# All modulation vectors through TensorE in four column groups, and a first FFN whose products begin with half of the scale

## Chip, cores and metric

The kernel runs on one core of a Trainium2 chip. The metric is device time in microseconds (us), the median of several executions. Six things work side by side on the core: TensorE (PE in the rows; its weight loads are PEld), VectorE (DVE), ScalarE (ACT), GpSimd (POOL), SyncE (SP, which issues nearly all DMAs) and the DMA engines. Every engine takes its own instructions strictly in the order in which the program lists them.

## Reference

One step of a two-layer trunk on 384 tokens (128 of a prompt, 256 of a sample), width 1024, all in float32. Each layer adds three branches to the residual x, every one with a norm that a conditioning modulates:

```python
mod = (jnp.einsum('bd,de->be', jax.nn.silu(cond), lp['w_ada']) + lp['b_ada']).reshape(cond.shape[0], N_MOD, 1, D_MODEL)
h = rms_norm(x, lp['norm_g'][0]) * (1.0 + mod[:, 1]) + mod[:, 0]
x = x + 0.5 * mod[:, 2] * swiglu(h, lp['ffn_w_gate'][0], lp['ffn_w_up'][0], lp['ffn_w_down'][0])
h = rms_norm(x, lp['norm_g'][1]) * (1.0 + mod[:, 4]) + mod[:, 3]
mix, state = token_mix(h, lp, l, cache)
x = x + mod[:, 5] * mix
h = rms_norm(x, lp['norm_g'][2]) * (1.0 + mod[:, 7]) + mod[:, 6]
x = x + 0.5 * mod[:, 8] * swiglu(h, lp['ffn_w_gate'][1], lp['ffn_w_up'][1], lp['ffn_w_down'][1])
```

`swiglu` is `silu(h @ w_gate) * (h @ w_up) @ w_down` with a hidden width of 2816. There are nine modulations of 1024 a layer, each for two conditionings (prompt and sample): `w_ada` is 1024 x 9216 for each layer, 37.7 MB a layer. The four mixers are not touched by the change.

## The kernel before, in words

**Layout.** Activations lie feature-major: 8 blocks of 128 features, 384 tokens in the free dimension. A large product is made with three fp32r matmuls (`mm3`, L184 to L188): weight and activation are split into a high and a low part (`whi`, `wlo`; `hhi`, `hlo`), and high by high, high by low and low by high are added in PSUM. The split costs one cast on ScalarE (L169) and one subtraction on VectorE (L173; GpSimd for a few) for each 128 x 1024 unit of weights. TensorE can't begin the third of the three before `wlo` is there.

**FFN.** There are four, called FFN 1 to 4 here: two in each layer, before and behind the mixers. One has a gate/up stage (44 units of 24 matmuls, tiles `pg` and `pu`, 1056 matmuls) and a down stage (tile `pd`, 528 matmuls). Weights come in MB pieces (`raw`, three buffers).

**Modulations.** All but five quarters run beside TensorE (`ada`, L258 to L292): a quarter is 256 of a modulation's 1024 columns, 1 MB of `w_ada`. For the prompt's conditioning, VectorE multiplies and adds eight blocks (L268, L271); for the sample's, ScalarE multiplies (L269, L274) and GpSimd adds (L275). Two 32 x 32 transposes (L278), two sums (L279) and, once for a group of quarters, four products with selection matrices (L285) bring the result to columns. These jobs are woven into the FFNs by `hook`: 28 quarters in FFN 1, 20 in FFN 2, 16 in FFN 3, none in FFN 4. The five others (`ada_rows`, L238 to L255) use TensorE at the start: the conditioning is the stationary operand (128 x 2), 256 columns of `w_ada` move, eight plain-fp32 products to a quarter (L246), then two transposes.

**Start.** The first norm needs modulation 1 (scale) and 0 (shift) of layer 0. `start` (L372) runs through `ORDER`: quarters of scale on TensorE, quarters of shift on the other engines, and between them the scaled residual `xs` (L345, L346). The first FFN's first ten products (`EARLY`) use `xs` with two extra columns that hold the shift (`early_shift`, L327), so that 386 columns move; the product is multiplied by 1/rms and shifted behind it (`hidden`, L194). So the first of them waits for the whole scale and the whole shift.

**Order.** The program is written in Python against a scheduler that simulates the engines' time and lists the instructions of each engine by it; jobs from `hook` carry a raised priority. What it lists is fixed before the launch.

Of the kernel before, what the change touches and what calls it, by code (L numbers as in the profile page):

```python
# [8 lines left out]
F32 = mybir.dt.float32  # L9
# [8 lines left out]
D = 1024  # L18
# [16 lines left out]
K_ID, K_SEL, K_ONE = 0, 128, 640  # L35
# [8 lines left out]
ORDER = "nsrsrsrrr"  # L44
RING, NT1, NT2 = 256 * 310, 6, 4
# [4 lines left out]
def host_constants():  # L50
# [12 lines left out]
    for r in range(4):  # L63
        c[:, K_SEL + 128 * r:K_SEL + 128 * (r + 1)] = i[None, :] == (32 * r + i[:, None] % 32)
# [15 lines left out]
def pack_vectors(x):  # L80
    """The small vectors of both layers as columns of 128."""
    import numpy as np

    rows = [x["c_ctx"].reshape(8, 128), x["c"].reshape(8, 128)]
    for l in range(2):
        rows += [x["norm_g"][l].reshape(24, 128), x["b_ada"][l].reshape(72, 128), x["dn_conv_w"][l].reshape(18, 128)]
        rows += [np.tile(x[n][l], 2)[None] for n in ("dn_norm_g", "da_norm_g", "ml_norm_g", "ret_norm_g")]
        rows.append(np.repeat(x["ret_decay_logit"][l].reshape(4, 2), 64, axis=1))
    return np.ascontiguousarray(np.concatenate(rows, 0).T)
# [6 lines left out]
def lockstep(*tasks):  # L96
    """Issue several tasks a stage of each at a time."""
# [5 lines left out]
class Ring:  # L103
    """Tiles at consecutive offsets of one window of memory, each over the oldest ones."""
# [13 lines left out]
class Trunk:  # L118
# [75 lines left out]
    def hidden(self, w, name="mm"):  # L194
        """A product with the normed residual; the first ones are scaled by 1 / rms and shifted behind the product."""
# [9 lines left out]
        nc.vector.tensor_copy(b, ps[:, T:T + 2])  # L205
        t = self.ring.tmp([128, T], "hn")
# [6 lines left out]
    def setup(self):  # L213
# [10 lines left out]
        nc.scalar.activation(out=self.cond, in_=vec[:, 0:16], func=AF.Silu)  # L224
        xrs = []
# [12 lines left out]
    def ada_rows(self, l, quarters):  # L238
        """Quarters of the nine modulations on the tensor engine, for both conditionings."""
        nc = self.nc  # L240
        cond = self.cond.rearrange("p (s k) -> p k s", s=2)
        for mod, j in quarters:
            raw = self.wcols(self.I["w_ada"][l], mod * D + 256 * j)
            ps = self.pm.tile([2, 256], F32, tag="mm", name="arow")
            for kk in range(KD):
                nc.tensor.matmul(ps, cond[:, kk], raw[:, kk], start=(kk == 0), stop=(kk == KD - 1))  # L246
            row = self.ring.tmp([2, 256], "mrow")
            nc.scalar.copy(row, ps)
            tp = self.mxps([128, 2, 2])
            for q in range(2):  # L250
                nc.tensor.transpose(tp[:, q], row[:, 128 * q:128 * q + 128], self.k(K_ID)[0:2, 0:2])
            c = slice(8 * mod + 2 * j, 8 * mod + 2 * j + 2)
            nc.vector.tensor_tensor(self.mods[l][:, :, c].rearrange("p s k -> p k s"), tp,
                                    self.prm[l][:, R_B:R_B + 72][:, c].unsqueeze(2).to_broadcast([128, 2, 2]),
                                    op=ALU.add)  # L255
            yield

    def ada(self, l, mod, n=4):  # L258
        """The same beside the tensor engine, n quarters from a modulation on, one at a time."""
        nc = self.nc  # L260
        ap = self.ap
        xa = ap.tile([128, 2, 8 * n], F32, tag="xa", name="xa", bufs=1)
        for j in range(n):
            raw = ap.tile([128, KD, 256], F32, tag="araw", name="araw", bufs=2)
            c0 = mod * D + 256 * j
            nc.sync.dma_start(raw, self.I["w_ada"][l, :, c0:c0 + 256].rearrange("(k p) n -> p k n", p=128))
            acc = [ap.tile([128, 256], F32, tag="acc", name="acc", bufs=6) for _ in range(2)]
            nc.vector.tensor_scalar_mul(acc[0], raw[:, 0], self.cond[:, 0:1])  # L268
            nc.scalar.mul(acc[1], raw[:, 0], self.cond[:, 8:9])  # L269
            for kk in range(1, KD):  # L270
                nc.vector.scalar_tensor_tensor(  # L271
                    acc[0], raw[:, kk], self.cond[:, kk:kk + 1], acc[0], op0=ALU.mult, op1=ALU.add)
                t = ap.tile([128, 256], F32, tag="acc", name="acct", bufs=6)
                nc.scalar.mul(t, raw[:, kk], self.cond[:, 8 + kk:9 + kk])  # L274
                self.last_add = nc.gpsimd.tensor_tensor(acc[1], acc[1], t, op=ALU.add)  # L275
            for s in range(2):
                tr = ap.tile([128, 256], F32, tag="acc", name="accr", bufs=6)
                nc.vector.transpose(tr, acc[s])  # L278
                nc.vector.tensor_reduce(  # L279
                    xa[:, s, 8 * j:8 * j + 8], tr.rearrange("p (a b) -> p a b", b=32), axis=AX, op=ALU.add  # L280
                )
            yield
        ps = self.mxps([128, 2, 2 * n])
        for r in range(4):
            nc.tensor.matmul(  # L285
                ps, self.k(K_SEL + 128 * r), xa.rearrange("p s (k r) -> p s k r", r=4)[:, :, :, r],
                start=(r == 0), stop=(r == 3),
            )
        c = slice(8 * mod, 8 * mod + 2 * n)
        nc.vector.tensor_tensor(self.mods[l][:, :, c], ps,  # L290
                                self.prm[l][:, R_B:R_B + 72][:, c].unsqueeze(1).to_broadcast([128, 2, 2 * n]), op=ALU.add)
        yield  # L292

# [8 lines left out]
    def norm_begin(self, l, n):  # L302
        """The statistics of the next norm gather while the residual is updated."""
# [22 lines left out]
    def early_shift(self):  # L326
        """Two columns beside the scaled residual, for the shift of the two streams behind the product."""  # L327
# [30 lines left out]
    def rstd(self):  # L358
        """1 / rms of every token, on all partitions."""
# [12 lines left out]
    def start(self):  # L372
        """The first norm, as the input and the quarters of its modulation come in."""
        self.norm_begin(0, 0)
        for kk in range(KD):
            self.norm_square(kk)
        self.early_open()
        shift, rows = self.ada(0, 0, ORDER.count("s")), self.ada_rows(
            0, [(1, j) for j in range(4)] + [(0, j) for j in range(ORDER.count("s"), 4)])
        j = 0  # L380
        for c in ORDER:
            if c == "n":
                self.rstd()
            elif c == "s":
                next(shift)
            else:
                next(rows)
                if j < 4:
                    self.scales(0, 0, self.nx[2], 2 * j, 2 * j + 2)
                    self.early_part(2 * j, True)  # L390
                    self.early_part(2 * j + 1, True)
                j += 1
        next(shift)
        self.early_shift()
        with self.after(self.last_add):
            for k in range(KD):
                self.norm_scale(k)
# [1087 lines left out]
```

## Time and profile before

| | us |
|---|---|
| median of 3 runs (2241.5 to 2248.05) | 2246.99 |
| span of the profiled execution | 2244.0 |
| start, up to the first product of FFN 1 | 48.6 |
| FFN 1, gate/up and down | 215.8 + 118.2 |
| FFN 2 | 216.3 + 111.3 |
| FFN 3 | 200.5 + 91.6 |
| FFN 4 | 186.0 + 94.8 |

The span runs from the first to the last instruction; the timed runs hold 3.0 us more by their median. Between the FFNs lie the mixers of layer 0 and layer 1. A view of stretches gives, for each, its length, then the busy time (and the instructions) of PE, PEld, DVE, ACT and POOL, the granted TensorE clock as a share of 2.4 GHz, the DMA share and GB/s. Matmuls overlap in TensorE's pipeline: one lasts twice as long as the distance to the next, so the distance between starts is read, not the duration. A plain-fp32 product stands in the trace as two MATMULs, two passes. An fp32r product is one.

### The profile page before, as it was taken

The numbers are of one execution on the slowest core, as the hardware profiler recorded it, in microseconds if no ns is written. First come the engines' busy times: TensorE is split into PE (matmuls) and PEld (weight loads), VectorE is DVE, ScalarE is ACT, GpSimd is POOL, SyncE is SP. The second block draws the span as 40 slices with busy tenths as digits, with TensorE's granted clock in tenths as the row PEclk, the third lists the DMA queues.
The fourth block names the chain that finished last, engine by engine and source line by source line (L and its number), as shares of the span: only waits on it lengthen the run. The fifth ranks groups of instructions, "written<-read, shape, count | busy, mean of one in ns | idle before, by whom it ended". The sixth has DMA issues, their size and how long they took to land. (4 is left out here: it accounts for less than half of the span.)

```text
span 2244.0 us, 33102 instructions
## 1 busy us (share of the span) xinstructions
PE 2076.3 (93%) x12150; PEld 1992.7 (89%) x12150; DVE 1724.6 (77%) x3198; ACT 1039.3 (46%) x1978; POOL 942.2 (42%) x855
## 2 busy tenths in 40 slices
PE   6988888999789997998998999999987999999999
PEld 3988788999679997998887999998976899999999
DVE  8999998778995469999899974467999745764433
ACT  5666554634234235765556643354333332463322
POOL 5556666433655237366476520134354531500000
PEclk8999999999889999999999999999998999999999
DMA  9466655444333244566555644344442321444342
GB/s 306 152 217 199 202 198 164 129 136 105 83 81 103 60 164 155 169 210 214 186 193 155 206 135 133 128 146 137 119 95 83 109 76 59 160 134 129 115 139 76
DMA packets 316515, 323.08 MB, mean 144 GB/s; under 512 B 42112, under 2 KB 287296, under 8 KB 315840
## 3 DMA queue, kind: packets, MB, share of 16 engines
q1 hardware_dynamic: 316080, 320.70, 46.1%
q8 instruction: 95, 1.56, 0.3%
q14 instruction: 68, 0.56, 0.1%
q10 hardware_dynamic: 272, 0.26, 0.0%
HBM read 313.25 MB, written 7.69 MB: 143 GB/s over the span
## 5 line engine op out<-in xcount | busy, mean ns | idle before, releaser
L169 ACT CAST whi<-raw 128x1024 fp32r<-128x1024 f32 x422 | 440.2, 1045 | 511.1 <-PE mg L187 133.3
L173 DVE TENSOR_TENSOR wlo<-raw,whi 128x1024 fp32r<-128x1024 f32 x324 | 434.8, 1343 | 226.9 <-ACT whi L169 223.8
L275 POOL TENSOR_TENSOR acc<-acc,acct 128x256 f32<-128x256 f32 x469 | 440.5, 939 | 334.7 <-ACT acct L274 306.4
L173 POOL TENSOR_TENSOR wlo<-raw,whi 128x1024 fp32r<-128x1024 f32 x98 | 244.9, 2505 | 289.9 <-ACT whi L169 244.2
L271 DVE SCALAR_TENSOR_TENSOR acc<-araw,cond,acc 128x256 f32<-128x256 f32 x469 | 323.5, 690 | 6.3
L274 ACT ACTIVATE acct<-araw,cond 128x256 f32<-128x256 f32 x469 | 214.1, 501 | 139.7 <-DVE accr L278 83.4
L188 PE MATMUL pd<-hh,wlo 128*128 128x384 f32 x704 | 240.8, 345 | 20.2 <-DVE wlo L173 20.2
L186 PE MATMUL pd<-hh,whi 128*128 128x384 f32 x704 | 240.5, 342 | 9.0 <-ACT whi L169 4.5
L187 PE MATMUL pd<-hl,whi 128*128 128x384 f32 x704 | 239.9, 341 | 0.0
L188 PE MATMUL pg<-hhi,wlo 128*128 128x384 f32 x544 | 184.8, 340 | 19.2 <-DVE wlo L173 19.0
L188 PE MATMUL pu<-hhi,wlo 128*128 128x384 f32 x544 | 184.7, 340 | 13.4 <-DVE wlo L173 13.1
L186 PE MATMUL pg<-hhi,whi 128*128 128x384 f32 x544 | 182.1, 335 | 0.4 <-ACT whi L169 0.4
L187 PE MATMUL pu<-hlo,whi 128*128 128x384 f32 x544 | 182.2, 335 | 0.0
L186 PE MATMUL pu<-hhi,whi 128*128 128x384 f32 x544 | 182.2, 335 | 0.0
L187 PE MATMUL pg<-hlo,whi 128*128 128x384 f32 x544 | 182.1, 335 | 0.0
L186 PE MATMUL mg<-hhi,whi 128*128 128x384 f32 x512 | 177.7, 347 | 0.0
L187 PE MATMUL mg<-hlo,whi 128*128 128x384 f32 x512 | 175.4, 343 | 0.0
L188 PE MATMUL mg<-hhi,wlo 128*128 128x384 f32 x512 | 174.5, 343 | 0.5 <-DVE wlo L173 0.5
L321 POOL TENSOR_SCALAR xg<-xT,gs 128x128 f32<-128x128 f32 (+1 forms) x96 | 101.9, 1074 | 150.9 <-DVE xT L432 150.8
L188 PEld LDWEIGHTS pd<-hh,wlo 128*128 128x128 f32 x704 | 134.0, 191 | 27.6 <-DVE wlo L173 27.6
L186 PEld LDWEIGHTS pd<-hh,whi 128*128 128x128 f32 x704 | 134.4, 191 | 11.3 <-ACT whi L169 5.4
L187 PEld LDWEIGHTS pd<-hl,whi 128*128 128x128 f32 x704 | 134.5, 191 | 0.1
(410 smaller groups left out, 4961.5 us busy)
## 6 DMA issues: line engine op xcount, KB each, us to landing
araw<-in_w_ada SPq DMA_DIRECT2D x67, 1024.0 KB
raw<-in_w_in SPq DMA_DIRECT2D x62, 1024.0 KB
raw<-in_ffn_w_gate SPq DMA_DIRECT2D x44, 1024.0 KB
raw<-in_ffn_w_up SPq DMA_DIRECT2D x44, 1024.0 KB
raw<-in_ffn_w_down SPq DMA_DIRECT2D x40, 1024.0 KB
raw<-in_w_branch SPq DMA_DIRECT2D x16, 512.0 KB
raw<-in_w_out SPq DMA_DIRECT2D x8, 1024.0 KB
raw<-in_w_ada SPq DMA_DIRECT2D x5, 1024.0 KB
```

Of the source, the lines that this page charges most:

```text
L169: nc.scalar.copy(hi, src)
L173: (eng or nc.vector).tensor_tensor(lo, src, hi.bitcast(F32), op=ALU.subtract)
L186: nc.tensor.matmul(ps, w[0], x[0], start=start, stop=False)
L187: nc.tensor.matmul(ps, w[0], x[1], start=False, stop=False)
L188: nc.tensor.matmul(ps, w[1], x[0], start=False, stop=stop)
L271: nc.vector.scalar_tensor_tensor(acc[0], raw[:, kk], self.cond[:, kk:kk + 1], acc[0], op0=ALU.mult, op1=ALU.add)
L274: nc.scalar.mul(t, raw[:, kk], self.cond[:, 8 + kk:9 + kk])
L275: self.last_add = nc.gpsimd.tensor_tensor(acc[1], acc[1], t, op=ALU.add)
L321: self.nc.gpsimd.tensor_scalar(xg[kk][:, a:e], self.xT[:, kk, a:e], gs[:, s, kk:kk + 1], None, op0=ALU.mult)
```

## The change

Every modulation now goes through TensorE. A half (512 of 1024 columns) is loaded as two 1 MB tiles (`araw`). `pair_rows_times` takes the conditionings as a stationary of 128 x 32 (`cond32`: two columns used, thirty zero) and sends 512 columns of a block of 128 rows past it; block `kk` stands in column group `kk % 4` of the array, 32 columns wide, and writes 32 partitions of one PSUM tile (`arow`). Eight such products make a half, two for each group. ScalarE copies the tile, four transposes (`acol`) turn it, and one sum on VectorE adds the four groups; the bias is added behind. The code of the other engines (`ada`, `ada_rows`, the selection matrices) is gone.

The halves are woven into the FFNs one at each `hook`: 12 in FFN 1, 8 in FFN 2, 10 in FFN 3, 2 in FFN 4. Four stand at the start. There, six units of FFN 1 are begun without the shift columns: the first four blocks of three units when the first half of the scale is known, the other four when the second is, then three whole units; the shift's halves come after them. What the shift adds to these six units is a product of its own, of the raw weights with the shift (`sh32`, again in four column groups, 256 columns), added as a bias behind (`shifted`). The scales of the next norm are computed later, between the two halves of the down stage.

```diff
-K_ID, K_SEL, K_ONE = 0, 128, 640
+K_ID, K_ONE = 0, 128
...
-ORDER = "nsrsrsrrr"
-RING, NT1, NT2 = 256 * 310, 6, 4
+EARLY0 = 6
+RING, NT1, NT2 = 256 * 308, 6, 4
...
+        return self.shifted(ps, b)
+
+    def shifted(self, ps, b):
+        nc = self.nc
...
+        self.cond32 = self.const.tile([128, KD, 32], F32, name="cond32")
+        nc.vector.memset(self.cond32, 0.0)
+        nc.vector.tensor_copy(self.cond32[:, :, 0:2], self.cond.rearrange("p (s k) -> p k s", s=2))
...
-    def ada_rows(self, l, quarters):
...
-    def ada(self, l, mod, n=4):
...
+    def ada_load(self, l, mod, hf):
+        c0 = mod * D + 512 * hf
+        raws = []
+        for i in range(2):
+            raws.append(self.ap.tile([128, 4, 512], F32, tag="araw", name="araw", bufs=self.n_araw))
+            self.last_load = self.nc.sync.dma_start(raws[i], self.I["w_ada"][l, 512 * i:512 * i + 512, c0:c0 + 512].rearrange(
+                "(k p) n -> p k n", p=128))
+        return raws
+    def pair_rows_times(self, cols, blocks, n, out):
+        nc = self.nc
+        ps = self.mxps([128, n], "arow")
+        for kk in range(KD):
+            g = kk % 4
+            nc.tensor.matmul(ps[32 * g:32 * g + 32], cols[:, kk], blocks[kk], start=(kk < 4), stop=(kk >= 4),
+                             tile_position=(0, 32 * g))
+        row = self.ring.tmp([128, n], "mrow")
+        nc.scalar.copy(row, ps)
+        tp = self.mxps([128, n // 128, 128], "acol")
+        for q in range(n // 128):
+            nc.tensor.transpose(tp[:, q], row[:, 128 * q:128 * q + 128], self.k(K_ID))
+        nc.vector.tensor_reduce(out, tp.rearrange("p q (g e) -> p e q g", g=4)[:, 0:2], axis=AX, op=ALU.add)
+    def ada_half(self, l, mod, hf, raws):
+        t = self.small.tile([128, 2, 4], F32, tag="asum", name="asum")
+        self.pair_rows_times(self.cond32, [r[:, g] for r in raws for g in range(4)], 512, t)
+        c = slice(8 * mod + 4 * hf, 8 * mod + 4 * hf + 4)
+        self.nc.vector.tensor_tensor(self.mods[l][:, :, c], t,
+                                     self.prm[l][:, R_B:R_B + 72][:, c].unsqueeze(1).to_broadcast([128, 2, 4]), op=ALU.add)
+    def ada(self, l, *halves):
+        for h in halves:
+            self.ada_half(l, *h, self.ada_load(l, *h))
...
+        wg, wu = I["ffn_w_gate"][0, 0], I["ffn_w_up"][0, 0]
+
+        def cols(w, c0):
+            t = self.ring.tile([128, KD, 256], F32, name="raw0")
+            nc.sync.dma_start(t, w[:, c0:c0 + 256].rearrange("(k p) n -> p k n", p=128))
+            return t
+
+        scale = [self.ada_load(0, 1, 0)]
+        raw = [cols(wg, 0), cols(wu, 0)]
+        scale.append(self.ada_load(0, 1, 1))
+        raw.append(self.wcols(wg, 256))
+        shift = [self.ada_load(0, 0, hf) for hf in range(2)]
+        self.up1 = self.wcols(wu, 256)
+        sh32 = self.ring.tile([128, KD, 32], F32, name="sh32")
+        nc.gpsimd.memset(sh32, 0.0)
+        units = [(0, 0), (1, 0), (0, 1), (1, 1), (2, 0), (2, 1)]
+        w, ps = {}, {}
+
+        def split(u):
+            r, m = u
+            w[u] = self.split_unit(raw[r][:, :, 128 * m:128 * m + 128], [128, KD, 128])
+            ps[u] = (self.mmps if r < 2 else lambda name: self.mxps([128, T], name))(name="pg" if r != 1 else "pu")
+
+        def rows(u, k0, k1):
+            for k in range(k0, k1):
+                self.mm3(ps[u], (w[u][0][:, k], w[u][1][:, k]), [t[:, k, 0:T] for t in self.xs], k == 0, k == KD - 1)
+
+        for hf in range(2):
+            self.ada_half(0, 1, hf, scale[hf])
+            self.scales(0, 0, self.nx[2], 4 * hf, 4 * hf + 4)
+            for k in range(4 * hf, 4 * hf + 4):
+                self.early_part(k, True)
+            if hf == 0:
+                for u in units[:3]:
+                    split(u)
+                    rows(u, 0, 4)
+        for u in units[:3]:
+            rows(u, 4, KD)
+        self.rstd()
+        for u in units[3:]:
+            split(u)
+            rows(u, 0, KD)
+        for hf in range(2):
+            self.ada_half(0, 0, hf, shift[hf])
+        nc.vector.tensor_copy(sh32[:, :, 0:2], self.mods[0][:, :, 0:8].rearrange("p s k -> p k s"))
+        bias = []
+        for r in range(3):
+            bias.append(self.small.tile([128, 2, 2], F32, tag="sb", name="sb", bufs=3))
+            self.pair_rows_times(sh32, [raw[r][:, kk] for kk in range(KD)], 256, bias[r])
...
+        self.ready = [(ps[u], bias[u[0]][:, :, u[1]]) for u in units]
...
+        if (l, n) == (0, 0):
+            self.early = EARLY0
...
+            begun = 2 - j if (l, i) == (0, 0) and j < 2 else 0
+            rg = None if begun else self.wcols(I["ffn_w_gate"][l, i], 256 * j)
+            ru = None if begun == 2 else self.up1 if begun else self.wcols(I["ffn_w_up"][l, i], 256 * j)
...
+                pg = self.shifted(*self.ready.pop(0)) if begun else self.hidden(wg, "pg")
+                pu = self.shifted(*self.ready.pop(0)) if begun == 2 else self.hidden(wu, "pu")
...
-            hook(2)
+            hook(1)
...
+            if nxt is not None and dg == 0:
+                self.scales(*nxt, self.nx[2])
...
+            self.n_araw = 4
...
+            self.n_araw = 3
...
-                self.ffn(l, 0, self.ada(l, 5, 16) if l else chain(self.ada(l, 2, 12), self.ada(l, 5, 16)), (l, 1))
+                mods = {(0, 0): ((0, 2, 8),), (0, 1): ((0, 8, 9), (1, 0, 3)), (1, 0): ((1, 3, 8),), (1, 1): ((1, 8, 9),)}
+                jobs = [chain(*(self.ada(m, *((k, hf) for k in range(a, e) for hf in range(2)))
+                                for m, a, e in mods[l, i])) for i in range(2)]
+                self.ffn(l, 0, jobs[0], (l, 1))
...
-                self.ffn(l, 1, iter(()) if l else self.ada(1, 0, 20), None if l else (1, 0))
+                self.ffn(l, 1, jobs[1], None if l else (1, 0))
```

Where the scheduler puts this: the first place is TensorE at the start (`arow` is a modulation's row tile, `mx` a small product or a transpose, `pg` and `pu` are the FFN's products). Before:

```order
L246 MATMUL arow_386<-raw_384,cond_89 2x256 x8
L246 MATMUL arow_413<-raw_411,cond_89 2x256 x8
L251 MATMUL mx_397<-cst_82,mrow_395 128x2 x2
L251 MATMUL mx_424<-cst_82,mrow_422 128x2 x2
L285 MATMUL mx_428<-xa_182,cst_82 128x12 x4
L186 MATMUL pg_519<-xs_160,whi_511 128x386
```

Now:

```order
L261 MATMUL arow_192<-araw_165,cond32_91 32x512 x4
L261 MATMUL arow_192<-araw_167,cond32_91 32x512 x4
L267 MATMUL acol_203<-cst_82,mrow_201 128x128 x4
L184 MATMUL pg_232<-xs_163,whi_228 128x384
L185 MATMUL pg_232<-xs_164,whi_228 128x384
```

The first FFN product stood behind five quarters and the shift; it now stands behind one half of the scale, whose eight products are in one row.

The second place is TensorE in FFN 1's gate/up stage, where `hook` puts a half. Before:

```order
L187 MATMUL pg_1222<-hlo_461,whi_1214 128x384
L188 MATMUL pg_1222<-hhi_460,wlo_1215 128x384
L186 MATMUL pu_1247<-hhi_460,whi_1218 128x384
L187 MATMUL pu_1247<-hlo_461,whi_1218 128x384
L188 MATMUL pu_1247<-hhi_460,wlo_1219 128x384
```

Now:

```order
L261 MATMUL arow_950<-araw_945,cond32_91 32x512
L184 MATMUL pu_1070<-hhi_572,whi_1041 128x384
L261 MATMUL arow_950<-araw_945,cond32_91 32x512
L185 MATMUL pu_1070<-hlo_573,whi_1041 128x384
L261 MATMUL arow_950<-araw_947,cond32_91 32x512
L186 MATMUL pu_1070<-hhi_572,wlo_1042 128x384
```

A product of 32 columns and one of the FFN's take turns, one by one, until the eight of the half are through.

The third place is VectorE in the same stage. Before:

```order
L173 TENSOR_TENSOR wlo<-raw,whi 128x1024
L271 SCALAR_TENSOR_TENSOR acc<-araw,cond,acc 128x256
L468 TENSOR_TENSOR hl<-sg,hh 128x384
L271 SCALAR_TENSOR_TENSOR acc<-araw,cond,acc 128x256 x2
L278 STREAM_TRANSPOSE accr<-acc 128x256
L173 TENSOR_TENSOR wlo<-raw,whi 128x1024
```

Now:

```order
L493 TENSOR_TENSOR sg<-sg,pu 128x384
L171 TENSOR_TENSOR wlo<-raw,whi 128x1024
L497 TENSOR_TENSOR hl<-sg,hh 128x384
L171 TENSOR_TENSOR wlo<-raw,whi 128x1024
L268 TENSOR_REDUCE asum<-acol 128x8
L274 TENSOR_TENSOR mods_87<-asum,vec 128x2x4
```

The multiply-adds between the splits are gone; one sum and one addition to a half are left.

How the list puts the 256 thin products (32 columns, `w_ada`) of the four FFNs among the full ones:

| | alone between full products | three in a row | five in a row (4 + 1) | eight in a row |
|---|---|---|---|---|
| FFN 1 (12 halves) | 82 | 2 times | | 1 time |
| FFN 2 (8 halves) | 54 | | 2 times | |
| FFN 3 (10 halves) | 72 | | | 1 time |
| FFN 4 (2 halves) | 6 | | 2 times | |

## Rows read from the trace of the kernel before

**Rows 1.** Stretches: length, PE, PEld, DVE, ACT, POOL, clock, DMA; FFN 1 to 4.

```profile
48.60:264.40 215.80, 195.35 (x1066) 185.99 (x1066) 212.04 (x350) 136.75 (x270) 131.77 (x138) 0.99 0.62 197
264.40:382.60 118.20, 102.50 (x537) 97.13 (x537) 109.99 (x182) 63.38 (x116) 79.57 (x86) 0.94 0.57 182
864.80:1081.10 216.30, 194.60 (x1067) 188.00 (x1066) 211.33 (x348) 135.31 (x265) 122.96 (x128) 0.98 0.58 186
1081.10:1192.40 111.30, 97.70 (x538) 93.48 (x537) 99.00 (x161) 58.71 (x109) 69.50 (x73) 0.98 0.60 196
1192.40:1392.90 200.50, 191.65 (x1075) 188.07 (x1074) 155.82 (x256) 106.92 (x197) 66.78 (x66) 0.98 0.49 153
1392.90:1484.50 91.60, 91.60 (x531) 91.60 (x530) 39.28 (x58) 30.75 (x39) 13.84 (x20) 1.00 0.43 129
1958.20:2144.20 186.00, 185.26 (x1067) 184.90 (x1066) 94.81 (x145) 80.22 (x130) 7.90 (x6) 1.00 0.40 125
2144.20:2239.00 94.80, 94.80 (x549) 94.45 (x548) 31.65 (x38) 23.28 (x25) 0.00 (x0) 1.00 0.28 97
```

**Rows 2.** Groups of instructions on DVE during FFN 1: busy us, mean ns, idle before.

```profile
L271 DVE SCALAR_TENSOR_TENSOR acc<-araw,cond,acc 128x256 f32<-128x256 f32 x196 | 135.0, 689 | 2.6
L173 DVE TENSOR_TENSOR wlo<-raw,whi 128x1024 fp32r<-128x1024 f32 x66 | 97.0, 1472 | 0.4 <-ACT whi L169 0.4
```

**Rows 3.** Waits of PE during FFN 1: us in total, times, longest.

```profile
PE pg L188 <- DVE wlo L173: 11.6, 13, 2.1
PE pd L188 <- DVE wlo L173: 11.5, 11, 2.1
```

**Rows 4.** A stretch within FFN 3's down stage, columns as in rows 1.

```profile
1402.50:1458.60 56.10, 56.10 (x325) 56.10 (x324) 23.37 (x30) 17.34 (x22) 7.14 (x8) 1.00 0.39 128
```

**Rows 5.** Timeline, PE: one product with 32 rows of stationary between full ones.

```profile
611.49 0.34 PE L188 MATMUL mg<-hhi,wlo 128*128 128x384 f32 x1
611.76 0.91 PE L1057 MATMUL mx<-bkTs,bqT 32*128 32x384 f32 x2
612.60 0.45 PE L186 MATMUL mg<-hhi,whi 128*128 128x384 f32 x1
612.88 0.34 PE L187 MATMUL mg<-hlo,whi 128*128 128x384 f32 x1
```

**Rows 6.** Timeline, PE: two quarters of a modulation (sixteen products, 32 passes).

```profile
23.24 7.07 PE L246 MATMUL arow<-raw,cond 128*2 128x256 f32 x32
```

**Rows 7.** Groups of weight loads from 20 to 30 us: busy us, mean ns.

```profile
L246 PEld LDWEIGHTS arow<-raw,cond 128*2 128x2 f32 x37 | 3.1, 85 | 4.7 <-issue 0.2
L363 PEld LDWEIGHTS mx<-cst,sqacc 128*128 128x128 f32 x6 | 0.7, 191 | 1.5 <-PE arow L246 1.5
```

**Rows 8.** Timeline, PE: a plain-fp32 product of full width between full ones.

```profile
1101.39 0.45 PE L285 MATMUL mx<-xa,cst 128*128 128x80 f32 x2
1101.56 0.46 PE L186 MATMUL pd<-hh,whi 128*128 128x384 f32 x1
1101.86 0.45 PE L285 MATMUL mx<-xa,cst 128*128 128x80 f32 x2
```

**Rows 9.** Timeline, PE: three products in three row groups, one behind another.

```profile
607.91 0.92 PE L1057 MATMUL mx<-bkTs,bqT 32*128 32x384 f32 x6 [0.37 <-DVE bkTs L1044]
```

**Rows 10.** Timeline, PE: four transposes between full products.

```profile
576.91 0.60 PE L1042 MATMUL mx<-cst,bx 128*128 128x128 f32 x4
577.26 0.42 PE L186 MATMUL mg<-hhi,whi 128*128 128x384 f32 x1
```

**Rows 11.** Stretches of the start, columns as in rows 1.

```profile
0.00:10.00 10.00, 3.50 (x17) 3.12 (x18) 1.78 (x3) 1.50 (x2) 0.19 (x4) 1.00 0.83 275
10.00:20.00 10.00, 5.15 (x20) 2.06 (x19) 9.52 (x15) 6.47 (x15) 5.73 (x7) 0.66 1.10 349
```

**Rows 12.** Timeline, PE: the first FFN product; then a stretch as in rows 1.

```profile
48.60 0.69 PE L186 MATMUL pg<-xs,whi 128*128 128x386 f32 x1 [3.34 <-ACT xs L332]
49.00:69.00 20.00, 19.05 (x97) 18.54 (x97) 19.07 (x37) 13.07 (x31) 17.35 (x16) 0.87 0.55 175
```

More of the change, by code (lines that the diff above doesn't have):

```diff
@@ L62, in host_constants @@
     c[:, K_PB:K_PB + 128] = 128 - i[None, :]
-    for r in range(4):
-        c[:, K_SEL + 128 * r:K_SEL + 128 * (r + 1)] = i[None, :] == (32 * r + i[:, None] % 32)
     c[:, K_KP] = 127 - i
@@ L235, in setup @@
                 nc.vector.tensor_copy(self.xT[:, 4 * hf:4 * hf + 4, 128 * b:128 * b + 128], tp)
-    def ada_rows(self, l, quarters):
-        nc = self.nc
[L241 to L255, printed above, removed]
-            yield
@@ L258, in ada @@
-    def ada(self, l, mod, n=4):
[L260 to L292, printed above, removed]
@@ L372, in start @@
     def start(self):
+        nc, I = self.nc, self.I
         self.norm_begin(0, 0)
@@ L377, in start @@
         self.early_open()
[L378 to L392, printed above, removed]
@@ L393, in start @@
-        next(shift)
-        self.early_shift()
-        with self.after(self.last_add):
-            for k in range(KD):
-                self.norm_scale(k)
+        wg, wu = I["ffn_w_gate"][0, 0], I["ffn_w_up"][0, 0]
[5 more added lines that the diff above has]
+        raw = [cols(wg, 0), cols(wu, 0)]
@@ L398, in start @@
+        self.ready = [(ps[u], bias[u[0]][:, :, u[1]]) for u in units]
+        for k in range(KD):
+            self.norm_scale(k)
         self.norm()
@@ L453, in ffn_body @@
         for j in range(KF // 2):
-            rg = self.wcols(I["ffn_w_gate"][l, i], 256 * j)
-            ru = self.wcols(I["ffn_w_up"][l, i], 256 * j)
+            begun = 2 - j if (l, i) == (0, 0) and j < 2 else 0
+            rg = None if begun else self.wcols(I["ffn_w_gate"][l, i], 256 * j)
+            ru = None if begun == 2 else self.up1 if begun else self.wcols(I["ffn_w_up"][l, i], 256 * j)
             for m in range(2):
                 f = 2 * j + m
-                wg = self.split_unit(rg[:, :, 128 * m:128 * m + 128], [128, KD, 128])
-                wu = self.split_unit(ru[:, :, 128 * m:128 * m + 128], [128, KD, 128])
-                pg = self.hidden(wg, "pg")
-                pu = self.hidden(wu, "pu")
+                wg = None if begun else self.split_unit(rg[:, :, 128 * m:128 * m + 128], [128, KD, 128])
+                wu = None if begun == 2 else self.split_unit(ru[:, :, 128 * m:128 * m + 128], [128, KD, 128])
+                pg = self.shifted(*self.ready.pop(0)) if begun else self.hidden(wg, "pg")
+                pu = self.shifted(*self.ready.pop(0)) if begun == 2 else self.hidden(wu, "pu")
                 sg = self.wp.tile([128, T], F32, tag="nt", name="sg", bufs=2)
@@ L473, in ffn_body @@
             self.norm_begin(*nxt)
-            self.scales(*nxt, self.nx[2])
         g = self.gates(l, 2 * i, 0.5)
```

## The prediction

> **What bounds the kernel now.** I read the stretches of the four FFNs first [rows 1], since they hold 55% of the span and all of the modulation work. All four run the same 1056 and 528 products. Where nothing holds TensorE up, it starts one each 56.1 / 325 = 0.173 us [rows 4]. FFN 4 has no modulation work and takes 186.0 + 94.8 us, with VectorE busy for half of its gate/up stage; the down stage of FFN 3, whose quarters have run out, takes 91.6. So 186.0 + 91.6 = 277.6 us is a clean FFN with a norm behind it. FFN 1 takes 334.0, FFN 2 327.6, FFN 3 292.1: they lose 56, 50 and 15 us. The cause is VectorE: in FFN 1 it is busy for 322 of 334 us, 135.0 of them with the multiply-adds of the quarters, and a split (L173) takes 1472 ns beside them [rows 2]. TensorE waits for the low part of the weights, in the gate/up and in the down stage [rows 3]; the listed waits are less than the loss, because products that start late overlap less. The fourth place is the start: the first FFN product stands at 48.6, after waiting 3.34 us for the shift columns [rows 12]. What the change can win is these 121 us and part of the 48.6.
>
> **What it removes.** The multiply-adds leave VectorE, ScalarE and GpSimd in FFN 1 to 3. With those 196 gone, VectorE has at most 322 - 135 = 187 us of work in FFN 1, and I set the three FFNs at their clean 277.6.
>
> **What it adds: the price of a thin product.** In the listed order 214 of the 256 thin products in the FFNs stand alone between full ones, twice three stand in a row, and six times five or eight. A pass of 256 plain-fp32 columns costs 7.07 / 32 = 0.22 us [rows 6], so two passes of 512 cost 0.88, whether 2 or 128 columns of the array are used. Four groups would share that only if their products stood side by side. The nearest thing in the trace to a thin product between full ones is one with 32 rows of stationary [rows 5]: from the full product before it to the one behind the next there are 612.88 - 611.49 = 1.39 us where two distances of 0.173 would have been 0.35, so it adds 1.04. Its two passes of 384 columns are 0.66 of that, and 0.38 is the price of going into a tiled shape and out of it, with weight loads that nothing hides. One of these loads will be of 32 columns, not 128: by 85 ns for 2 columns and 191 for 128 [rows 7] it is 0.08 shorter. A thin product alone costs 0.88 + 0.38 - 0.08 = 1.18 us. Bounds: 0.88 if going in and out is free; 1.04 by a plain-fp32 product of full width between full ones (0.17 to the next one, which then holds 0.30 and not 0.17; its passes of 80 columns are 0.14, so 0.16 is lost) [rows 8]; 1.26 with nothing off. I take 1.18, since rows 5 is the only one with a tiled shape, a full product on either side and wide passes.
>
> Products in a row can share: three in three row groups take 0.92 us together, one alone 0.91 [rows 9, 5]. So three thin ones in a row cost one, and five or eight cost two rounds: 1.76 + 0.30 = 2.06. No row shows column groups side by side; the other bound is that they run in turn (a rival below).
>
> The Trainium skill (TensorEngine Tiling (Array Packing), Key Properties) says that tiles take weights and products in parallel, and that changing the tiling mode, not just the tile, drains the engine. By its first half alone the 256 would cost 64 rounds of 0.88 with a few changes, about 65 us in place of 267, and the sum below would be near 2200; by its second half a full product in between costs a drain each time, which is what rows 5 show, and the listed order has one in between 214 times.
>
> Four transposes take 0.35 and leave the next load unhidden, 0.45 in all [rows 10]. Copy, sum and bias addition lie on ScalarE and VectorE, which now have room; if that cover were gone, they would cost nothing before a next norm needs them. The loads keep their bytes; a half is 2 MB, 6 us at 349 GB/s [rows 11], against some 28 us of gate/up work between two hooks, and the three buffers let one tile come early. On SyncE a load that waits for a buffer holds the next weights behind it for about half of the thin products' 11 us, which the three `raw` buffers cover.
>
> **The sum, against the span of 2244.0.**
> FFN 2: 54 x 1.18 + 2 x 2.06 = 67.8, transposes 8 x 0.45 = 3.6; 277.6 + 71.4 = 349.0 for 327.6: +21.4.
> FFN 3: 72 x 1.18 + 2.06 = 87.1, transposes 4.5; 369.2 for 292.1: +77.1.
> FFN 4: 6 x 1.18 + 2 x 2.06 = 11.2, transposes 0.9: +12.1 on 280.8.
> Start and FFN 1: input, constants and the first half are 3.9 MB; 2.75 MB have come after 10 us and the rest comes at 349 GB/s [rows 11], so it is there at 13. Two rounds at 1.2 GHz (the clock is at half for most of 10 to 20 us [rows 11]) take 3.5; copy, transposes, sum and scaling about 3 (my estimate): the first FFN product starts at 20. 36 products at half clock, 0.35 each, end at 33; the second half, landed at 25, and its scaling let the next 36 end at about 43; 72 more at 0.173 end at 56. The two halves of the shift, each 2.06 and a chain through ScalarE and VectorE behind it, and the shift columns take until 67 (57 to 77). By then 144 products are done. Before, 97 were done at 69 [rows 12] and 144 at about 77: the start wins 10, not 28, since the array is at half clock and waits for the shift later. Behind 67: 912 products, 157.4; three shift products of 256 columns (two rounds of 0.44, 0.30) with six transposes, 4.4; thin 84 x 1.18 + 2.06 = 101.2; transposes 5.4; down 91.6. FFN 1 ends at 427.0, before at 382.6: +44.4.
> Mixers: the same instructions in nearly the same order, nought.
> In all +155.0: 2399.0, and with the 3.0 by which the median stands over the span, **2402**. The break-even price of a lone thin product is 1.18 - 155 / 216 = 0.46 us.
>
> **The rivals.**
> *The chip brings the four groups together (faster).* If a queue ahead of the array lets the next group's thin product start beside the one before although a full one is listed between, four cost one, 0.30 each: 64.8 + 12.4 for 267, so 2402 - 190 = 2212. It decides below 0.46 us. For it: rows 9, where the first passes of three products stand together though each product has a second. Against it: a full product needs every column, so it can't start before the thin one ends, and in rows 5 the next full one started only when both passes were through. 7 in 100.
> The Trainium skill (TensorE: Matmul & The Clock Gate, What overlaps and what doesn't) says that matmuls start and end strictly in order; by that this rival gives nothing and the time stays at 2402.
> *Column groups don't share even in a row.* Then the longer rows in the FFNs cost 25 us more and the start 34 (10.6 of it at half clock ahead of the first product): 2461. 9 in 100.
> *The clock falls.* If thin products count as rest, the array goes to 1.2 GHz through each half: 216 x (0.88 + 0.17) = 227 more, 2629. Against it: at 23 us, with 2 columns, passes came at 0.22, the full clock's pace [rows 6]. 2 in 100.
> *Nearly free changes of shape and an earlier start:* 0.88 each and 57 at the start, 2325, still slower. Within the forecast's own range.
> *The change doesn't do what it says:* that four groups run one at a time is the forecast itself.
>
> **How the numbers follow.** The forecast, lone thin products at 0.88 to 1.26, holds 80 in 100: 2335 to 2421 from the price, with 10 either way from the start and as much for waits that stay in the FFNs. With the row rival's 2461 the range is 2325 to 2468; it leaves out the faster rival, the clock and the ends, some 18 in 100. Under 0.3%, about what a measurement of this kernel can tell from no change, lies between: 2 in 100 for a price near 0.46. Faster 7, slower 91.
>
> **What would show it.** In the profile after: `arow` products in FFN 2 alternating with full ones, 1.3 to 1.4 us from one to the next if 1.18 holds, 1.05 if only the passes count, under 0.5 if the rival is right; waits for `wlo` near nought and VectorE near half busy in FFN 1 to 3; FFN 3 near 369 us; the first FFN product near 20 us and a gap of TensorE near 60 to 67; four-in-a-row at the start in about 1.8 us at half clock. Wrong would make it: thin products that overlap full ones, full ones that still wait for the splits, or a lower clock in FFN 1 to 3.

## The result and the profile after

The changed kernel takes 2408.43 us (2407.45 to 2410.16) against 2247.52 us (2241.5 to 2250.13) before: a ratio of 1.0724, 95% interval 1.0709 to 1.074, so it is slower by 161 us. Its profiled execution has a span of 2405.4 us.

The stretches of the four FFNs, gate/up and down in turn, with the columns of [rows 1]:

```profile
19.70:324.00 304.30, 295.63 (x1376) 207.41 (x1377) 102.97 (x189) 93.09 (x160) 15.06 (x16) 0.98 0.53 180
323.90:431.40 107.50, 107.50 (x574) 94.97 (x573) 40.68 (x65) 31.30 (x41) 13.81 (x19) 1.00 0.38 121
912.10:1168.20 256.10, 256.10 (x1227) 196.60 (x1227) 95.17 (x163) 83.73 (x136) 5.42 (x4) 1.00 0.47 156
1168.20:1259.90 91.70, 91.70 (x530) 91.70 (x529) 37.98 (x49) 29.29 (x37) 11.70 (x14) 1.00 0.38 126
1259.80:1535.50 275.70, 275.70 (x1263) 199.23 (x1262) 96.19 (x165) 85.06 (x141) 7.37 (x5) 1.00 0.46 153
1535.50:1628.90 93.40, 93.40 (x535) 93.37 (x534) 39.77 (x61) 30.17 (x39) 13.83 (x19) 1.00 0.38 116
2108.20:2305.20 197.00, 197.00 (x1107) 187.28 (x1107) 94.14 (x148) 80.33 (x131) 5.83 (x4) 1.00 0.39 123
2305.20:2400.00 94.80, 94.80 (x549) 94.45 (x548) 31.68 (x38) 23.24 (x25) 0.00 (x0) 1.00 0.30 97
```

Read them beside [rows 1]. VectorE has come down from 212.04 to 102.97 us in the first stretch, and from 211.33 to 95.17 in the third; TensorE has no idle time left in FFN 2 to 4. Yet every gate/up stage is longer than before, FFN 3's by 75 us. The tell is the fourth column: weight loads were busy nearly all the time that TensorE was (188.07 of 191.65 in FFN 3 before) and are now busy for 199 of 276. TensorE is busy with something that loads few weights.

Two groups tell what it is (line, engine, operation, tiles, count; then busy us, mean ns; then idle before). The first is VectorE's split during FFN 1, as in [rows 2]; the second is TensorE's over the whole run:

```profile
L171 DVE TENSOR_TENSOR wlo<-raw,whi 128x1024 fp32r<-128x1024 f32 x67 | 81.7, 1224 | 99.8 <-ACT whi L167 81.6 <-PE pd L186 15.2 <-DMA rs<-in_state_ret 2.9
L261 PE MATMUL arow<-araw,cond 128*32 128x512 f32 x576 | 247.2, 609 | 1.8 <-DMA araw<-in_w_ada 1.6
```

The list of TensorE's waits has two on the low part of the weights in the whole run; those of [rows 3] alone were 23.1 us in FFN 1:

```profile
PE mg L186 <- DVE wlo L171: 0.5, 2, 0.2
PE pu L186 <- DVE wlo L171: 0.2, 1, 0.2
```

So the change does what it is written to do: VectorE is out of the way, and a split in FFN 1 no longer takes 1472 ns [rows 2] but 1224. The time went to the 32-column products. How it is spent shows only in the order of TensorE's timeline, in FFN 1 (start, length, engine, line, operation):

```profile
100.07 0.34 PE L185 MATMUL pu<-xs,whi 128*128 128x386 f32 x1
100.34 1.04 PE L261 MATMUL arow<-araw,cond 128*32 128x512 f32 x2
101.31 0.44 PE L186 MATMUL pu<-xs,wlo 128*128 128x386 f32 x1
101.69 1.05 PE L261 MATMUL arow<-araw,cond 128*32 128x512 f32 x2
102.66 0.44 PE L184 MATMUL pu<-xs,whi 128*128 128x386 f32 x1
103.03 1.05 PE L261 MATMUL arow<-araw,cond 128*32 128x512 f32 x2
```

From one thin product to the next there are 1.35 us (100.34, 101.69, 103.03) where one full product, 0.173, would have stood: each adds 1.17 us. Thin and full take turns, as the list has them. Where four thin ones stand together, at the start, the same view shows:

```profile
25.17 0.34 PE L185 MATMUL pg<-xs,whi 128*128 128x384 f32 x1
25.44 1.07 PE L261 MATMUL arow<-araw,cond 128*32 128x512 f32 x8
26.44 0.44 PE L186 MATMUL pu<-xs,wlo 128*128 128x384 f32 x1
```

Four products, eight passes, hold TensorE for 1.00 us (25.44 to 26.44); one alone holds it for 0.97 (100.34 to 101.31). So column groups do share the array, and almost fully, where they are neighbours in the list.

The start, in the same view:

```profile
14.22 1.82 PE L261 MATMUL arow<-araw,cond 128*32 128x512 f32 x8 [1.57 <-DMA araw<-in_w_ada]
16.81 1.11 PE L267 MATMUL acol<-cst,mrow 128*128 128x128 f32 x4 [0.76 <-ACT mrow L264]
19.73 0.69 PE L184 MATMUL pg<-xs,whi 128*128 128x384 f32 x1 [1.81 <-ACT xs L334]
...
61.60 1.92 PE L261 MATMUL arow<-araw,cond 128*32 128x512 f32 x16
64.23 0.66 PE L267 MATMUL acol<-cst,mrow 128*128 128x128 f32 x4 [0.71 <-ACT mrow L264]
68.56 0.66 PE L184 MATMUL pu<-xs,whi 128*128 128x386 f32 x2 [3.68 <-ACT xs L321]
```

The first FFN product stands at 19.73 in place of 48.60 [rows 12]. The 144 early ones are through at 58.4; then the shift goes through TensorE, and the next product stands at 68.56, behind a wait of 3.68 us for the shift columns.

### The profile page after: what moved, and what is told of

The parts are those of the page before. It is cut to its first block, busy times and chain, and to the rows that moved or that the text cites. A ratio compares the mean times of both kernels' runs of the same rounds, so it can differ in the third digit from the quotient of the medians.

```text
span 2405.4 us, 32241 instructions
## 1 busy us (share of the span) xinstructions
PE 2316.9 (96%) x12794; PEld 2029.0 (84%) x12794; DVE 1267.5 (53%) x2456; ACT 839.5 (35%) x1480; POOL 493.2 (21%) x387
## 5 line engine op out<-in xcount | busy, mean ns | idle before, releaser
L171 DVE TENSOR_TENSOR wlo<-raw,whi 128x1024 fp32r<-128x1024 f32 x324 | 401.6, 1240 | 456.1 <-ACT whi L167 437.3
L310 POOL TENSOR_SCALAR xg<-xT,gs 128x128 f32<-128x128 f32 (+1 forms) x96 | 93.1, 984 | 1052.1 <-DVE xT L460 1029.1
L261 PE MATMUL arow<-araw,cond 128*32 128x512 f32 x576 | 247.2, 609 | 1.8 <-DMA araw<-in_w_ada 1.6
L493 DVE TENSOR_TENSOR sg<-sg,pu 128x384 f32<-128x384 f32 x67 | 37.1, 554 | 339.6 <-PE pu L186 339.6
L185 PE MATMUL pu<-hlo,whi 128*128 128x384 f32 x536 | 188.8, 352 | 0.0
L186 PE MATMUL pg<-hhi,wlo 128*128 128x384 f32 x536 | 179.1, 334 | 0.0
L186 PEld LDWEIGHTS pu<-hhi,wlo 128*128 128x128 f32 x536 | 100.6, 188 | 59.5 <-issue 59.5
L185 PEld LDWEIGHTS pu<-hlo,whi 128*128 128x128 f32 x536 | 100.6, 188 | 58.7 <-issue 58.7
L184 PEld LDWEIGHTS pu<-hhi,whi 128*128 128x128 f32 x536 | 100.5, 188 | 41.1 <-issue 41.1
```

The lines of the kernel that those rows point to most:

```text
L171: (eng or nc.vector).tensor_tensor(lo, src, hi.bitcast(F32), op=ALU.subtract)
L184: nc.tensor.matmul(ps, w[0], x[0], start=start, stop=False)
L185: nc.tensor.matmul(ps, w[0], x[1], start=False, stop=False)
L186: nc.tensor.matmul(ps, w[1], x[0], start=False, stop=stop)
L261: nc.tensor.matmul(ps[32 * g:32 * g + 32], cols[:, kk], blocks[kk], start=(kk < 4), stop=(kk >= 4), tile_position=(0, 32 * g))
L310: self.nc.gpsimd.tensor_scalar(xg[kk][:, a:e], self.xT[:, kk, a:e], gs[:, s, kk:kk + 1], None, op0=ALU.mult)
```

## The experiments

Theory: the loss is the price of lone thin products; in a row they share, and the change would win. Rivals: TensorE loses the time to something else that came with the change (the transposes, the loads, the start), or the price lies in the tile position as such. Ratios are against the kernel before on the same chip (2245.8 us; 2245.31 for the full-width product, the shift ahead of the last early units and the kernel before without its modulations).

**Thin products in one row.** The eight of a half get ranks that are meant to put them side by side; nothing else is edited.

```diff
+            with self.tc.high_priority(offset=3 * kk):
-            nc.tensor.matmul(ps[32 * g:32 * g + 32], cols[:, kk], blocks[kk], ...
+                nc.tensor.matmul(ps[32 * g:32 * g + 32], cols[:, kk], blocks[kk], ...
```

> The changed kernel with one thing different: the eight thin products of a half get nearly the same rank with the scheduler, so that they stand in one row and not in turns with full products. Theory (a lone thin product costs 1.17 us, its two passes and the way into and out of the tiled shape; four groups in a row share): 216 lone ones at 1.17 and 6 longer rows at 2.06 become 32 rows of eight at 2.06, so 266 us become 66 to 70 and the time is about 2211 us, below the kernel before. Rival 1 (the price goes by passes, whatever stands side by side): the rows save only the changes of shape, 216 x 0.3 = 65, about 2343. Rival 2 (with TensorE quicker, VectorE's splits are late again): 2211 plus some of the 121 us of waits of before, 2230 or more.

Measured: 2206.42 us (2204.44 to 2208.47), ratio 0.9825 (0.9812 to 0.9839). The same instructions in another order are 202 us faster, and faster than the kernel before by 39. In the trace 28 of the 32 halves of the FFNs stand in one row and four in two parts. A half in FFN 2 in the timeline, then the gate/up stages of FFN 2 and 3 as stretches:

```profile
884.55 0.34 PE L185 MATMUL pu<-hlo,whi 128*128 128x384 f32 x1
884.82 1.92 PE L262 MATMUL arow<-araw,cond 128*32 128x512 f32 x16
886.67 0.44 PE L186 MATMUL pu<-hhi,wlo 128*128 128x384 f32 x1
886.95 0.34 PE L184 MATMUL pu<-hhi,whi 128*128 128x384 f32 x1
```

```profile
832.20:1038.30 206.10, 206.10 (x1227) 191.21 (x1226) 97.72 (x164) 84.31 (x137) 6.73 (x5) 1.00 0.59 194
1129.90:1339.50 209.60, 209.60 (x1263) 192.37 (x1262) 97.36 (x165) 84.40 (x141) 7.36 (x5) 1.00 0.61 200
```

Eight thin products hold TensorE for 1.85 us and add 2.05 (from 884.55 to 886.95, less two full ones); 1227 matmuls in 206.10 us were the same 1227 in 256.10 under the change.

**No thin products.** What the four FFNs' modulations compute is left out (products, copies, transposes, sums); their loads and the start stay, and the modulation is the bias alone.

```diff
-        for h in halves:
-            self.ada_half(l, *h, self.ada_load(l, *h))
+        for mod, hf in halves:
+            self.ada_load(l, mod, hf)
+            ...
+            self.nc.vector.tensor_copy(self.mods[l][:, :, c], ...
```

> The changed kernel with the thin products, their copies, transposes and sums in the four FFNs left out: those modulations are set to their bias alone; their loads stay, and so does the start. It measures what they cost by themselves. Theory: 266 us for the thin products and 14 for the transposes, so about 2128 us, and TensorE without waits for the splits in all four FFNs. Rival (part of the time lies in loads or in VectorE and not in TensorE's turns): well over 2140.

Measured: 2126.68 us (2118.37 to 2127.88), ratio 0.9462 (0.9444 to 0.948). FFN 2 and FFN 3 as stretches:

```profile
801.30:987.20 185.90, 185.45 (x1067) 184.76 (x1067) 95.00 (x146) 79.09 (x128) 5.21 (x4) 1.00 0.83 286
987.20:1078.90 91.70, 91.70 (x530) 91.70 (x529) 38.00 (x49) 29.33 (x37) 11.77 (x14) 1.00 0.38 126
1078.70:1263.60 184.90, 184.90 (x1068) 184.86 (x1067) 96.33 (x147) 78.57 (x131) 6.92 (x5) 1.00 0.40 126
```

These are the clean FFNs, 185.9 + 91.7. The loads run beside the first of them more densely than under the change: nothing reads the loaded tiles here, so they come early, 26 of 1 MB during FFN 2's gate/up (286 GB/s) and none during FFN 3's (126 GB/s, what its own weights need). Under the change the modulation work of the FFNs is therefore worth 2408.4 - 2126.7 = 281.7 us, known to some 5 us by the two intervals; the prediction had 267.2 for the products and 14.4 for the transposes. In rows it is 79.7, or 2.49 a half (2.06 + 0.45 by the prediction's terms).

**One column group in place of four.** In the FFNs all eight products of a half add into the same 32 partitions, with no tile position; the stationary stays 32 columns wide.

```diff
+            ps = self.px.tile([32, n], F32, tag="mx", name="arow")
+            for kk in range(KD):
+                nc.tensor.matmul(ps, cols[:, kk], blocks[kk], start=(kk == 0), stop=(kk == KD - 1))
...
```

> The changed kernel, but in the FFNs a half's eight thin products use no column groups: the same 128 x 32 stationary in the array's ordinary shape, all eight added in one PSUM tile of 32 partitions. The turns with full products stay. Theory (half of the price of going in and out is the change of shape): from one lone thin product to the next 1.21 us where the changed kernel has 1.35, no time lost for all that the groups are gone: 2400 to 2410 us, since the rows of three and eight no longer share. Rival (the price belongs to plain fp32 beside fp32r, not to the shape): 1.35 from one to the next, about 2440 us.

Measured: 2435.69 us (2432.91 to 2438.47), ratio 1.0846 (1.0826 to 1.0866). The timeline in FFN 1:

```profile
159.85 1.04 PE L261 MATMUL arow<-araw,cond 128*32 128x512 f32 x2
160.83 0.45 PE L185 MATMUL pu<-hlo,whi 128*128 128x384 f32 x1
161.20 1.04 PE L261 MATMUL arow<-araw,cond 128*32 128x512 f32 x2
```

My expectation of 1.21 us from one to the next missed: it is 1.35, as under the change. The records give the shape as 128*32, which is the rows and columns in use ([rows 6] has 128*2). So the edit took away the four groups but not the narrow stationary, and did not settle what it was made for. It shows two other things. Going back and forth between groups costs nothing, since one group has the same distances. And the few rows of three, five and eight that the change does have are worth 27 us (2435.7 - 2408.4), for they no longer share here; the prediction's row rival had 25 for that.

**A full-width thin product.** As the last, but the stationary is padded with zeros to 128 columns and the result has 128 partitions, so that the number of columns in use never changes.

```diff
+            ps = self.mxps([128, n], "arow")
+            for kk in range(KD):
+                nc.tensor.matmul(ps, self.condw[:, kk], blocks[kk], start=(kk == 0), stop=(kk == KD - 1))
...
+            self.condw = self.ap.tile([128, KD, 128], F32, name="condw")
```

> As the kernel untiled, but the stationary is padded with zeros to 128 columns and the PSUM tile has 128 partitions, so that a thin product has the array's full shape; turns with full products stay, eight products add up in one tile. The kernel untiled still showed 1.35 us from one thin product to the next, as in the changed kernel: one group alone of 32 columns costs the same way in and out as four. Theory (the way in and out is paid for the 32-column shape): 1.21 us from one to the next, 30 us under untiled, about 2405. Rival (it is paid for plain fp32 between fp32r products): 1.35 or, with a wider weight load, 1.43; 2436 to 2455 us.

Measured: 2361.22 us (2355.58 to 2366.85), ratio 1.0515 (1.0486 to 1.0543), 44 us under what I expected. The timeline in FFN 1:

```profile
152.43 1.02 PE L261 MATMUL arow<-araw,condw 128*128 128x512 f32 x2
152.88 0.74 PE L185 MATMUL pu<-hlo,whi 128*128 128x384 f32 x1
153.46 1.02 PE L261 MATMUL arow<-araw,condw 128*128 128x512 f32 x2
153.92 0.74 PE L186 MATMUL pu<-hhi,wlo 128*128 128x384 f32 x1
154.49 1.02 PE L261 MATMUL arow<-araw,condw 128*128 128x512 f32 x2
```

From one to the next there are 1.03 us, of which 0.17 are the full product's and 0.86 the two passes of 512 columns: going in and out costs nothing. So the other 0.31 of a lone thin product belong to the 32-column shape. In the trace of the change they lie at three places: 0.20 ahead of the first pass (0.37 from the full product, not 0.17), 0.03 between the passes (0.45, not 0.43) and 0.09 behind the second (0.52, not 0.43).

The weight loads differ too. Under the change, then at full width:

```profile
101.68 0.14 PEld L261 LDWEIGHTS arow<-araw,cond 128*32 128x32 f32 x2 [0.19 <-issue]
102.66 0.19 PEld L184 LDWEIGHTS pu<-xs,whi 128*128 128x128 f32 x1 [0.84 <-issue]
```

```profile
153.29 0.36 PEld L261 LDWEIGHTS arow<-araw,condw 128*128 128x128 f32 x2 [0.24 <-issue]
153.89 0.19 PEld L186 LDWEIGHTS pu<-hhi,wlo 128*128 128x128 f32 x1 [0.24 <-issue]
```

With 32 columns the first load of the next product starts only with that product (101.68 for the thin one at 101.69, 102.66 for the full one at 102.66); at full width it starts ahead of it, while the product before still runs (153.29 for the thin one at 153.46, 153.89 for the full one at 153.92).

The Trainium skill (TensorEngine Tiling (Array Packing), Key Properties) says that changing the tiling mode drains the engine. The trace agrees so far that a lone product of another shape costs 0.31 us over its passes and one of the same shape none. Whether the late loads are the cause of those 0.31 or follow from a drain, no run here tells, nor whether 32 columns without a tile position count as another mode.

**No early units.** As the thin products in one row, and the new start goes too: scale and shift first, all on TensorE, and then the ten products with shift columns as before.

```diff
-            if hf == 0:
-                for u in units[:3]:
-                    split(u)
-                    rows(u, 0, 4)
...
         self.early_shift()
...
-            self.pair_rows_times(sh32, [raw[r][:, kk] for kk in range(KD)], 256, bias[r])
...
-            begun = 2 - j if (l, i) == (0, 0) and j < 2 else 0
+            begun = 0
```

> The kernel in_row with the other half of the change undone: no unit of FFN 1 is begun ahead of the shift; the first ten products carry the two shift columns as in the kernel before, behind both halves of the scale and of the shift, all on TensorE. Theory (the head start is mostly spent on half clock, on the later wait for the shift and on three shift products): 5 to 12 us over in_row. Rival (the head start counts in full): 20 to 28 us over in_row.

Measured: 2203.24 us (2197.48 to 2203.99), ratio 0.981 (0.9796 to 0.9823). It should have been 5 to 12 us slower than the products in one row with the new start, and is level with it or 3 faster. FFN 1 begins at 43.37 here and at 18.86 there, but ends at 350.19 here and at 355.64 there. Counted from the trace, the FFN products started by 60, 70 and 100 us are 94, 150 and 293 here, and 144, 148 and 267 there. The head start of 50 products at 60 us is gone ten us later. This late start isn't the start of the kernel before: with all modulations on TensorE its first product stands at 43.37 and not at 48.60, and by 60 us it has started 94 products where the kernel before has 46. The stretch of those ten us with the new start, and the wait in it:

```profile
60.00:70.00 10.00, 5.23 (x36) 2.37 (x29) 10.00 (x29) 6.08 (x17) 0.00 (x0) 0.69 0.78 289
```

```profile
PE pu L184 <- ACT xs L322: 4.1, 1, 4.1
```

VectorE is busy for all of it, with the normed residual (`xg`, `hlo`), the begun units (`hn`) and, between them, the short steps from the shift's rows to the shift columns; TensorE is busy for half, at a mean clock of 0.69. In place of the 58 products that fit (10 / 0.173), four are made.

**The shift ahead of the last early units.** As the thin products in one row; only the order of the start is edited, so that two begun units stand behind the shift and cover that chain.

```diff
-        for u in units[3:]:
+        for u in units[3:4]:
...
         nc.vector.tensor_copy(sh32[:, :, 0:2], ...
+        for u in units[4:]:
+            split(u)
+            rows(u, 0, KD)
```

> The kernel in_row with the start in another order: the two halves of the shift, and the shift columns made from them, come ahead of the last two begun units of FFN 1 and not behind them. In in_row TensorE has done 144 products at 60 us and then does hardly anything up to 69, for want of the shift columns (a wait of 4.1 us and the chain of copy, transposes and sums around it); in_row_late, which begins nothing early, has as many products at 70. Theory (that hole eats the head start): the last 48 products cover it, 5 to 9 us under in_row, 2198 to 2202 us. Rival (the hole only moves, since the chain hangs on the landing of the shift's loads or on VectorE's queue): within 2 us of in_row, 2205 to 2208.

Measured: 2201.23 us (2197.92 to 2203.65), ratio 0.9801 (0.9787 to 0.9814), 5 us below the products in one row. The same ten us, and those behind:

```profile
60.00:70.00 10.00, 10.00 (x78) 8.38 (x77) 4.71 (x10) 5.96 (x13) 0.00 (x0) 1.00 0.31 100
70.00:80.00 10.00, 10.00 (x74) 7.57 (x73) 5.83 (x11) 5.10 (x10) 0.00 (x0) 1.00 0.54 174
```

The wait is gone, the clock is whole, and FFN 1 ends at 347.40. This has the lowest ratio of the versions that compute everything, 44 us under the kernel before, but it can't be told apart from the start without early units (ratio 0.981, 0.9796 to 0.9823).

**Before, without its modulations in the FFNs.** The multiply-adds, transposes and sums of the FFNs' quarters are left out, the loads and the old start stay; the modulation is the bias alone.

```diff
+    def none(self, l, mod, n):
+        for j in range(n):
+            ...
+            self.nc.sync.dma_start(raw, self.I["w_ada"][l, :, c0:c0 + 256].rearrange("(k p) n -> p k n", p=128))
+            yield
...
-                self.ffn(l, 0, self.ada(l, 5, 16) if l else chain(self.ada(l, 2, 12), self.ada(l, 5, 16)), (l, 1))
+                self.ffn(l, 0, self.none(l, 5, 16) if l else chain(self.none(l, 2, 12), self.none(l, 5, 16)), (l, 1))
...
```

> The kernel before with the modulations of the four FFNs left out (set to their bias; their loads stay), its start unchanged. Beside no_thin it sets the two starts against each other with nothing else between them. My sum had the new start 10 us ahead and 4 us of shift products behind: 5 to 8 us over no_thin, 2132 to 2135 us, FFN 1 to 3 at about 278 us each. Rival (the head start counts in full): 2150 or more. If VectorE's multiply-adds are what FFN 1 to 3 lost their time to, this kernel is 113 to 121 us under the kernel before; if not, FFN 1 to 3 stay over 290.

Measured: 2124.91 us (2123.68 to 2126.96), ratio 0.9464 (0.9451 to 0.9476). So the modulation work of the FFNs costs 2245.3 - 2124.9 = 120.4 us before; the prediction had 121 for what the FFNs lose. The gate/up stages of FFN 1 and 2:

```profile
48.40:236.10 187.70, 186.72 (x1057) 186.21 (x1058) 91.04 (x132) 76.77 (x123) 10.89 (x9) 0.98 0.88 278
807.40:992.30 184.90, 184.90 (x1067) 184.87 (x1067) 95.56 (x146) 79.53 (x130) 6.34 (x4) 1.00 0.94 299
```

The edit takes the work off ScalarE and GpSimd as well as off VectorE. That VectorE was the one that mattered rests on [rows 2] and [rows 3], and on the waits for `wlo`, of which this run has none in FFN 1.

I had expected 5 to 8 us over the version with the new start and no thin products; the two ratios (0.9464 and 0.9462) can't be told apart, and their intervals (3 and 4 us either way) just reach 5. In the profiles FFN 1 ends at 327.86 with the old start and at 324.03 with the new one; whether those 3.8 us are in the whole time can't be seen at this width.

## Why the prediction came out right, and where it was off

The forecast was 2402 us with a range of 2325 to 2468; 2408.4 was measured, and nearly every term of the sum came out as it stands there.

- **VectorE was the bound, and the clean FFN 277.6.** Right: 120.4 us of loss measured for 121, and 185.9 + 91.7 without thin products. What VectorE keeps is 143.7 us in FFN 1, at most 187 had been said; its share is 35% there, not near half, because the stage grew.
- **The price of a lone thin product, 1.18 us.** Measured 1.17: the passes are 0.86, not 0.88, and in and out 0.31, not 0.30. [rows 5] was the right row to take. The argument for the bound by [rows 8] was not: a full-width plain-fp32 product of 512 columns loses nothing, where I read 0.16 from passes of 80. That a pass of 80 columns is too short to hide the next load (0.19 by [rows 7]) would explain it, but is only argued.
- **A row, 2.06, and transposes, 0.45.** 2.49 a half for the sum, 2.51 predicted.
- **FFN 2, 3 and 4.** 349.0, 369.2 and 292.9 predicted; 347.8, 369.1 and 291.8 measured, each from its first product to its last.
- **The start and FFN 1.** First product at 20, measured 19.73; the next ones behind the shift at 67, measured 68.56; end at 427.0, measured 431.4. This is the term that was mis-sized. Behind the gap the sum has full clock, but the granted clock was 0.57 from 68.5 to 72.3: the first of the shift's three products holds TensorE for 1.86 us (69.63 to 71.49), the second, at full clock, for 1.00 (75.84 to 76.84). This slower stretch is about 1.6 us (3.8 x 0.43, an estimate) and the later shift columns are 1.6, together 3 of the 4.4 us. The step "the start wins 10", less 4.4 for the shift's products, left 5.6; the runs show 3.8 at the end of FFN 1, and in the total no difference that can be told from nought. I saw the gap at 60 to 67 but not that a start with no early units and all modulations on TensorE would come out level, because it has no gap and no products of its own for the shift.
- **The mixers, nought.** Layer 0's are 1.5 us shorter, layer 1's 5.6 longer. Over the nine profiles of this study layer 1's take from 473.7 to 483.9 us and layer 0's from 476.5 to 482.3 with the same work. Layer 1's granted clock is 0.97 before, 0.96 under the change and 0.95 in the longest (the full-width product), so some of it goes with the clock; why that differs, no run shows.
- **Sum.** +44.4, +21.4, +77.1 and +12.1 predicted; +48.8, +20.2, +77.0 and +11.0 by the profile (FFN 1 from the span's start), and 4.1 from the mixers: 161.1, and 161.4 between the spans.
- **The rivals.** The chip doesn't bring the groups together: thin and full products took turns wherever the list had them so (214 alone in the trace, as in the list). Column groups share in a row: 1.00 us for four, 0.97 for one. The clock stayed whole: 1.00 from FFN 1's down stage on, in the stretches shown.

Why the list takes turns was not in the prediction, and it is only argued: I read it as the rank that `hook` gives a woven job, which would put its eight thin products level with the full ones around it, one by one. What is shown is that the first experiment edits the ranks of the eight and nothing else, that most halves then stand in one row, and that this moved 202 us.

## What to carry to other kernels

Products in separate column groups saved time here only where nothing of another shape was listed between them, so the order that a scheduler really lists has to be read before the array's sharing is put into a sum. A narrow product that must stand alone between full ones may be cheaper padded to the full shape, as it was here (0.86 us added in place of 1.17). Work that is begun early is worth only what the next wait does not give back: count the products done by a time behind that wait, not the time of the first.

## What the hardware showed that I had not expected

- A plain-fp32 product of 512 columns in the full shape, set alone between fp32r products, adds its two passes and nothing else (0.86 us). With 32 columns of stationary it adds 1.17, with one group in use as with four.
- Four column groups share the array almost wholly: their first passes start 7 ns apart, and the four take 1.00 us for 0.97 of one. The Trainium skill (TensorEngine Tiling (Array Packing), Theoretical Speedup) gives up to 4 times for 32 columns; here it is 4 x 0.97 / 1.00, or 3.9.
- Loads cost the FFN's products nothing: 26 MB of `w_ada` came during FFN 2's gate/up without thin products, at a DMA share of 0.83, and it took 185.9 us, the clean stage.
